# FFN of a hybrid decoder layer in five wider token tiles, with w_down streamed through a ring of four blocks in place of staying in SBUF

## The chip, the cores and the metric

One Trainium2 chip, one program on all 8 cores; each core works on one of the 8 prompts and 16 of the 128 sample tokens, and reads all weights itself. The time is device microseconds of the slowest core. A run is called slow when the cores of one die are over 1% longer than those of the other at a lower clock, or when it is over 1.5% above the fastest of the same kernel; none is used, in the medians either. A ratio is the mean time of one kernel's fast runs over that of the other's fast runs of the same rounds, so it is not quite the ratio of the medians that are quoted beside it. The same kernel moved by up to 3 us between rounds, so two kernels of different rounds are compared by their ratios.

## The reference, cut to what matters (the comment is added)

```python
D_MODEL, D_FF, CONV_W = 1024, 2816, 3          # 2064 own tokens a core go through the FFN tiles
...
    # channel-mixing sub-layer: gated ConvFFN
    h = rmsnorm(x, g_pre_ffn)
    upc, new_ffn = causal_dwconv(h @ w_up, buf_ffn, w_ffn_conv)       # (B,T,2*D_FF)
    gate, val = jnp.split(upc, 2, axis=-1)
    y = (jax.nn.silu(gate) * val) @ w_down
    x = x + rmsnorm(y, g_post_ffn)
```

## The kernel before

A first stage (pooling and convolution mixers, 5 tiles "A") leaves h2, the normed input of the FFN, in a scratch tensor `h2T` in memory. The FFN (the layer's feed-forward part: w_up, a gate, w_down) takes 6 tiles of 344 tokens. A tile has 22 `pair`s (gate and value block of w_up, 2 x 8 matmuls of 346 columns, then convolution, silu and product) and 8 `wdown` blocks (22 matmuls each), which run one tile later, between the pairs of the next tile. All of w_down, 8 blocks of bf16, stays in SBUF, the core's on-chip memory, over the space of dead mixer weights. The weights are float32 in memory and bf16 in SBUF, so each of their loads is a casting DMA, issued from POOL. The outputs of all tiles but the last are added to what `yT` in memory holds, by accumulating stores from POOL. (The code is cut and its comments are added.)

```python
    W_DN = Buf(W_POOL.off, 8, FC * 128, True)      # 8 resident blocks
    H2W = NB + 8
    bl = Alloc(W_DN.end)
    h2a = bl(KC, H2W, True)                        # first h2 buffer, over two chunks of the pooled buffer
    TB = [bl(2, NB), bl(2, NB)]
    g0 = bl(FC, NB, True)
    ...
    def load_h2(t):
        lo = T0B + t * NB - 2
        hb = H2[t % 2]
        sp_dma(hb.ap[:, :, 0:NBH], h2T[:, :, lo:lo + NBH],
               [("h2", a, q) for a in tiles_a(lo, lo + NBH) for q in range(2)], [hb.t()], 128 * KC * NBH * 2)
    ...
    def wload(buf, src, m, after=()):              # float32 in memory, bf16 in SBUF: a casting DMA from POOL
        rows, per = buf.n // src.shape[0], src.shape[2]
        return pool_dma(buf.flat[:, m * per:(m + 1) * per], src[m], [], [buf.t(m * rows, rows)], 128 * per * 4, mx=2048,
                        after=after)
    ...
    for t in range(NTB):
        ...
        for j in range(FC):
            pair(t, j)
            if t == 0:
                wup(1)                             # one more block of w_up
            ...
            if (t, j) in ((0, 9), (0, 11), (0, 14), (0, 16), (0, 19), (0, 21), (1, 1), (1, 3)):
                wdn()                              # one w_down block, 8 in all
            wd = WD1 if t == 1 else WD
            if t > 0 and j in wd:
                wdown(t - 1, wd[j])
            if t > 1 and j == 0:
                epi_y(t - 2)                       # norm of a finished tile, accumulating stores to yT
    ...
    for m in range(8):
        wdown(NTB - 1, m, ...)                     # the tail: the last tile's own down-projection
```

A list scheduler inside the program orders the instructions of each engine; each engine has its instructions in that order, and so has the sync engine (SP) its DMAs.

## Time and profile before

| | before |
|---|---|
| time, median of 3 (later 4) runs | 823.04 (823.63) us |
| span of the profiled run, slowest core (the page is of a core of 816.0 us) | 816.4 us |
| PE busy, matmuls | 796.5 us, 5118 |
| w_down loads | 8 |
| transfers over the span | 93 GB/s |

In the page's strip of 40 slices, each digit is a busy share in tenths; PEclk is the granted TensorE clock.

```profile
PE   7999999999999999999999999999999999999994
PEclk9999999999999999999999999999999999999998
DMA  9999706567017699999990132015101500050073
```

### The profile page before, as it was taken

The page shows a single profiled execution, that of the slowest core. Times are in us where ns is not written, and L with a number is a line of the kernel's source. Part 1 is how long each engine was busy: PE and PEld are TensorE (multiplying, and loading weights), DVE is VectorE, ACT ScalarE, POOL GpSimd, SP SyncE. Part 2 cuts the span into 40 slices and gives each one's busy share as a digit, 9 for nine tenths or more (in the row PEclk, how much of TensorE's full clock was granted, in tenths as well). Part 3 has the DMA queues.
Part 4 walks back from the last instruction along what each step waited for, and adds up shares of the span by engine and source line. Part 5 has one row for each costly group of instructions (what it writes and reads, how often), then busy time and mean ns, then how long its engine had stood idle before and what let it go on. Part 6 is the DMA issues. An engine that isn't in the chain of part 4 may idle for free.

```text
span 816.0 us, 16713 instructions; the slowest of 8 cores (813.3 to 816.4 us)
## 1 busy us (share of the span) xinstructions
PE 796.5 (98%) x5118; PEld 498.2 (61%) x5118; DVE 562.4 (69%) x1056; ACT 451.9 (55%) x903; POOL 258.7 (32%) x296
## 2 busy tenths in 40 slices
PE   7999999999999999999999999999999999999994
PEld 5454455555555555666666666666666666666663
DVE  3897547886977687488886486568566765785732
ACT  3433375665465644676754475456556554765532
POOL 6542002001201243599432252225222522242231
PEclk9999999999999999999999999999999999999998
DMA  9999706567017699999990132015101500050073
GB/s 183 203 159 156 153 10 139 159 165 155 25 56 158 106 142 190 172 160 176 183 159 3 36 44 54 0 37 71 37 2 36 70 1 1 2 71 2 1 147 82
DMA packets 64006, 75.51 MB, mean 93 GB/s; under 512 B 3088, under 2 KB 59536, under 8 KB 63904
## 3 DMA queue, kind: packets, MB, share of 16 engines
q0 software_dynamic: 41168, 44.61, 38.8%
q1 hardware_dynamic: 22752, 29.84, 12.8%
q8 instruction: 43, 0.70, 0.3%
q14 instruction: 43, 0.35, 0.2%
HBM read 81.89 MB, written 22.90 MB: 128 GB/s over the span
## 4 chain that ended last, share of the span: by engine, by line
PE 94%; DMA 2%; DVE 1%; issue 1%; ACT 1%; DVEq 0%; POOL 0%; SPq 0%; ACTq 0%; POOLq 0%
PE ps L469 94%; DMA big<-w_in 1%; DMA big<-xT 1%; DVE big L549 0%; DVE big L821 0%; ACT big L817 0%; POOL big L482 0%; DVEq L1077 0%; ACT big L958 0%; DVE big L658 0%; DVE ps L869 0%; SPq L476 0%; DVE big L869 0%; DVE big L880 0%; DVE big L664 0%
## 5 line engine op out<-in xcount | busy, mean ns | idle before, releaser
L469 PE MATMUL ps<-big 128*128 128x346 bf16 (+5 forms) x5118 | 796.5, 319 | 9.0 <-DVE big L821 2.0
L469 PEld LDWEIGHTS ps<-big 128*128 128x128 bf16 x5118 | 498.2, 98 | 307.1 <-issue 12.9
L821 DVE SCALAR_TENSOR_TENSOR big<-ps,big 128x344 f32<-128x344 f32 (+1 forms) x528 | 281.1, 569 | 97.2 <-ACT big L817 75.1
L835 POOL TENSOR_TENSOR big<-big 128x344 bf16<-128x344 f32 x132 | 125.5, 952 | 259.2 <-DVE big L821 175.7
L817 ACT ACTIVATE big<-ps,big 128x344 f32<-128x344 f32 (+1 forms) x264 | 140.1, 541 | 71.3 <-PE ps L469 67.1
L834 ACT ACTIVATE big<-big 128x344 f32<-128x344 f32 x132 | 64.5, 489 | 44.2 <-DVE big L821 41.9
L700 ACT ACTIVATE big<-ps 128x392 f32<-128x392 f32 (+1 forms) x80 | 39.3, 513 | 55.5 <-PE ps L469 35.8
L480 POOL DMA_DIRECT2D big<-xT x16 | 14.9, 941 | 162.1 <-DVE big L713 148.6
L847 ACT ACTIVATE big<-ps,big 128x344 f32<-128x344 f32 x48 | 26.0, 546 | 55.5 <-PE ps L469 54.2
L482 POOL DMA_DIRECT2D big<-w_up x44 | 31.8, 727 | 53.3 <-PE ps L469 47.1
L713 DVE SCALAR_TENSOR_TENSOR big<-ps,big 128x392 f32<-128x392 f32 (+1 forms) x40 | 25.8, 645 | 31.2 <-PE ps L469 29.0
L509 DVE TENSOR_TENSOR big<-big 128x1568 bf16<-128x1568 bf16 (+3 forms) x28 | 23.6, 847 | 30.8 <-ACT big L732 28.9
L853 DVE TENSOR_TENSOR big<-big 128x688 bf16<-128x688 bf16 x17 | 8.8, 517 | 40.7 <-ACT big L850 40.7
L730 ACT ACTIVATE big<-ps,big 128x392 f32<-128x392 f32 (+1 forms) x40 | 24.5, 611 | 13.6 <-PE ps L469 13.5
L606 DVE TENSOR_TENSOR big<-big 128x406 f32<-128x406 f32 (+7 forms) x50 | 29.9, 600 | 1.5 <-ACT big L628 0.2
L480 POOL DMA_DIRECT2D yT<-big x20 | 26.2, 1550 | 12.9 <-DVE big L885 7.3
L482 POOL DMA_DIRECT2D big<-w_in x32 | 23.2, 749 | 20.1 <-DMA big<-w_in 11.5
L850 ACT ACTIVATE big<-ps 128x344 bf16<-128x344 f32 x48 | 21.6, 450 | 13.5 <-PE ps L469 13.5
L575 ACT ACTIVATE big<-big 128x392 f32<-128x392 f32 (+1 forms) x20 | 12.6, 637 | 29.1 <-DVE big L664 29.1
L549 DVE SCALAR_TENSOR_TENSOR big<-big 128x392 bf16<-128x392 f32 (+1 forms) x40 | 24.3, 647 | 5.9 <-ACT big L526 3.6
L578 DVE SCALAR_TENSOR_TENSOR big<-big 128x392 f32<-128x392 f32 (+1 forms) x40 | 25.5, 645 | 2.6 <-ACT big L575 2.1
L719 DVE TENSOR_TENSOR big<-big 128x392 bf16<-128x392 f32 (+1 forms) x40 | 24.7, 627 | 2.0
(62 smaller groups left out, 347.1 us busy)
## 6 DMA issues: line engine op xcount, KB each, us to landing
big<-w_up POOLq DMA_DIRECT2D x44, 256.0 KB, 18.4
big<-w_in POOLq DMA_DIRECT2D x32, 256.0 KB, 21.9
yT<-big POOLq DMA_DIRECT2D x20, 344.0 KB, 6.0
big<-xT POOLq DMA_DIRECT2D x16, 392.0 KB, 7.9
yT<-big SPq DMA_DIRECT2D x8, 784.0 KB, 9.2
big<-w_dn POOLq DMA_DIRECT2D x8, 704.0 KB, 28.6
big<-xT SPq DMA_DIRECT2D x6, 784.0 KB, 6.8
big<-h2T SPq DMA_DIRECT2D x6, 692.0 KB, 4.7
```

Source lines behind the costliest of these rows:

```text
L469: ins = e.matmul(o, lhsT=l, rhs=x, start=(start and i == 0), stop=(stop and i == last))
L480: return S.add("pool", lambda e: e.dma_start(out=out, in_=in_, accum_op=ALU.add, max_dma_last_dim=mx), r, w, dma=True, byts=byts, pri=pri, ...
L482: return S.add("pool", lambda e: e.dma_start(out=out, in_=in_, max_dma_last_dim=mx), r, w, dma=True, byts=byts, pri=pri, after=after)
L578: dve(lambda e, k=k: e.scalar_tensor_tensor(out=cv, in0=p[:, 2 + k + lo:2 + k + N], scalar=cc(C_WC + 4 * k + c), in1=cv, op0=ALU.mult, op1 ...
L606: dve(lambda e, nx=nx, cur=cur, s=s, a2=a2: e.tensor_tensor(out=nx[:, a2:W], in0=cur[:, a2:W], in1=cur[:, a2 - s:W - s], op=ALU.add), [ct] ...
L700: act(lambda e, b=b, g=g: e.activation(out=GT[t].ap[:, g, lo:N], in_=bank(b, N, lo), func=AF.Sigmoid), [("ps", b)], [GT[t].t(g, 1)], N, ps ...
L713: dve(lambda e: e.scalar_tensor_tensor(out=A_, in0=bank(bp, N, lo), scalar=cc(C_PS + m), in1=A_, op0=ALU.mult, op1=ALU.mult), [("ps", bp), ...
L817: act(lambda e, b=b, fj=fj, tt=tt: e.activation(out=tt[:, 0:n], in_=bank(b, n), func=AF.Copy, scale=cc(C_WF + fj)), [("ps", b), KCST], [to ...
L821: dve(lambda e, b=b, fj=fj, tt=tt, k=k: e.scalar_tensor_tensor(out=tt[:, 0:n], in0=ps[:, b * 512 + k:b * 512 + k + n], scalar=cc(C_WF + 44 ...
L834: act(lambda e: e.activation(out=g, in_=g, func=AF.Silu), [T.t(0, 1)], [T.t(0, 1)], NB, tab="silu")
L835: S.add("pool", lambda e: e.tensor_tensor(out=gb.ap[:, j, :], in0=g, in1=v, op=ALU.mult), [T.t()], [gb.t(j, 1)], dur=NB * 2.17 + 100)
L847: act(lambda e: e.activation(out=Y.ap[:, m, :], in_=bank(b, NB), func=AF.Copy, scale=cc(C_G4 + m)), [("ps", b), KCST], [Y.t(m, 1)], NB, ps ...
```

## The change

Its intent: fewer, wider matmuls (448 columns of a PSUM bank, which has 512 in this kernel), fewer fixed costs on all engines, and a short last tile so that the tail is short. The wider buffers fit only if w_down gives up half of its place: it passes through a ring of 4 blocks, a block's slot being filled with the block four further on as soon as its matmuls end. The last five blocks of the last tile go to five extra places, over w_up blocks that the last tile no longer needs. The core of the diff (cut: `N` for `NB` in many places, small temporaries moved, the h2 operations of the last A tile moved from pairs 20 to 29 to pairs 14 to 21):

```diff
-NTB = 6
-NB = 344
+TB_N = (448, 448, 448, 448, 272)
+OB = (0, 448, 896, 1344, 1792)
+NTB = 5
+NB = 448
...
-    W_DN = Buf(W_POOL.off, 8, FC * 128, True)
+    ring = Alloc(W_POOL.off)
+    W_DN = [ring(1, FC * 128, True) for _ in range(NR)]          # NR = 4
+    W_DNX = [Buf(W0 + 3 * BW * i, 1, FC * 128, True) for i in range(5)]
+    bl = Alloc(ring.o)
+    TB = [bl(2, NB)]
+    Y = bl(KC, NB)
+    TB.append(bl(2, NB))
     h2a = bl(KC, H2W, True)                    # now over three chunks of the pooled buffer
...
+    def wdn_buf(s):
+        return W_DN[s % NR] if s < 8 * NTB - 5 else W_DNX[s - (8 * NTB - 5)]
+
+    def wdn_load(s):
+        if s < 8 * NTB:
+            wload(wdn_buf(s), w_dn[s % 8:s % 8 + 1], 0, after=[last_pe[0]])
...
     def wdown(t, m, mid=None):
...
+        if s + NR < 8 * NTB - 5:                # s = 8 * t + m
+            wdn_load(s + NR)
...
+            if t == 0 and j in (12, 14, 16, 18):
+                wdn_load((j - 12) // 2)
+            if t == NTB - 1 and j in (7, 9, 11, 13, 15):
+                wdn_load(8 * NTB - 5 + (j - 7) // 2)
```

More of the change, by code (lines that the diff above doesn't have):

```diff
@@ L27 @@
 SCA = NA - NS
-NTB = 6
-NB = 344
-NBH = NB + 2
-SCB = NB - NS
+TB_N = (448, 448, 448, 448, 272)
+OB = (0, 448, 896, 1344, 1792)
+NTB = 5
+NB = 448
+NBL = TB_N[-1]
 T0B = 16
@@ L34 @@
 LOP = LO - 2
-SBW = 53200
+SBW = 53208
 GR = 4
@@ L377, in build_nc @@
     o_sq2 = al(KC, NMX, True).off
-    TMPF = al(4, NS)
+    al.o = SBW - 200 - 8 * NS
     STG = al(1, 200)
@@ L381, in build_nc @@
     assert al.o <= SBW, al.o
-    X = per_tile(KC, False, [o_x, W_O.off] + [o_x] * 3)
+    X = per_tile(KC, False, [o_x, W_O.off] + [o_cv + 5 * NA + 32] * 3)
     R = per_tile(KC, False, [o_r] + [X[2].end] * 4)
@@ L395, in build_nc @@
     PT = [Buf(o_pt, 2, UW), Buf(CV[1].end, 2, NA + 16)] + [Buf(CV[2].end, 2, NA + 16)] * 3
-    assert PT[2].end <= F_END and BGCV[1].end <= U.off and PT[1].end <= R[0].end
+    assert PT[2].end <= X[2].off and BGCV[1].end <= U.off and PT[1].end <= R[0].end
     ST_POOL = Buf(o_h2s, 4, 15 * NS)
@@ L410, in build_nc @@
     NMID = 12
+    NR = 4
     W_UP = Blocks([W0 + BW * i for i in range(16)] + [U.off + BW * i for i in range(NMID)] +
@@ L413, in build_nc @@
     assert U.off + BW * NMID <= F_END
-    W_DN = Buf(W_POOL.off, 8, FC * 128, True)
     H2W = NB + 8
-    bl = Alloc(W_DN.end)
+    ring = Alloc(W_POOL.off)
[5 more added lines that the diff above has]
+    TB.append(bl(2, NB))
     h2a = bl(KC, H2W, True)
-    TB = [bl(2, NB), bl(2, NB)]
     g0 = bl(FC, NB, True)
-    assert g0.end <= U.off
+    assert h2a.off >= MERGED[4].end and g0.end <= U.off, (h2a.off, g0.end)
     bl = Alloc(U.off + BW * NMID)
     g1 = bl(FC, NB, True)
-    Y = bl(KC, NB)
     YSQ = bl(4, NB, True)
     TB.append(Buf(SD.off + NMX, 2, NB))
-    bl = Alloc(max(bl.o, XSQ2[4].end))
+    TB.append(bl(2, NB))
+    TB.append(bl(2, NB))
+    assert bl.o <= XSQ2[4].end
+    bl = Alloc(XSQ2[4].end)
     h2b = bl(KC, H2W, True)
     PRE = bl(44, NS)
-    TB.append(bl(2, NB))
+    assert PRE.end <= STG.off
     H2, G = [h2a, h2b], [g0, g1]
@@ L432, in build_nc @@
     assert ST_FFN.end <= PRE.off and R[1].end <= ST_FFN.off + 1600
-    TAIL = Buf(h2a.off, 1, 44 * 18)
-    X1 = Buf(g0.off, KC, NB)
-    assert X1.end <= g0.end
+    TAIL = Buf(h2b.off, 1, 44 * 18)
+    X1 = Buf(g1.off, KC, NBL)
+    YB = [Y] * (NTB - 1) + [Buf(U.off, KC, NBL)]
+    assert X1.end <= g1.end
+    wd_use = [0]
+    def wdn_buf(s):
[3 more added lines that the diff above has]
+            wload(wdn_buf(s), w_dn[s % 8:s % 8 + 1], 0, after=[last_pe[0]])
     def cc(col, n=1):
@@ L613, in pool_c @@
                                              op0=ALU.mult, op1=ALU.subtract), [ct, U.t(c, 1)], [pd.t(c, 1)], N, stt=True)
-        tm = TMPF.ap[:, c, :]
+        tm = RED.ap[:, c, :]
         if t == 0 and w > LO:
@@ L617, in pool_c @@
                                           in1=CST[:, C_IC + 16 * c + lo:C_IC + 16 * c + 16],
-                                          op=ALU.mult), [ct, KCST], [TMPF.t(c, 1)], NS)
+                                          op=ALU.mult), [ct, KCST], [RED.t(c, 1)], NS)
             dve(lambda e: e.tensor_tensor(out=po[:, lo:16], in0=tm[:, lo:16], in1=u[:, 16 + lo:32], op=ALU.subtract),
-                [TMPF.t(c, 1), U.t(c, 1), pd.t(c, 1)], [pd.t(c, 1)], NS)
+                [RED.t(c, 1), U.t(c, 1), pd.t(c, 1)], [pd.t(c, 1)], NS)
         if last:
-            dve(lambda e: e.tensor_tensor(out=tm, in0=RED.ap[:, c, :], in1=u[:, 16 + SCA:W], op=ALU.add),
-                [RED.t(c, 1), U.t(c, 1)], [TMPF.t(c, 1)], NS)
+            dve(lambda e: e.tensor_tensor(out=tm, in0=tm, in1=u[:, 16 + SCA:W], op=ALU.add),
+                [RED.t(c, 1), U.t(c, 1)], [RED.t(c, 1)], NS)
             dve(lambda e: e.scalar_tensor_tensor(out=po[:, SCA:NA], in0=tm, scalar=1.0 / w, in1=u[:, 16 + SCA:W],
                                                  op0=ALU.mult, op1=ALU.subtract),
-                [TMPF.t(c, 1), U.t(c, 1), pd.t(c, 1)], [pd.t(c, 1)], NS)
+                [RED.t(c, 1), U.t(c, 1), pd.t(c, 1)], [pd.t(c, 1)], NS)
         else:
@@ L794, in load_h2 @@
     def load_h2(t):
-        lo = T0B + t * NB - 2
+        lo, n = T0B + OB[t] - 2, TB_N[t] + 2
         hb = H2[t % 2]
-        sp_dma(hb.ap[:, :, 0:NBH], h2T[:, :, lo:lo + NBH],
-               [("h2", a, q) for a in tiles_a(lo, lo + NBH) for q in range(2)], [hb.t()], 128 * KC * NBH * 2)
+        sp_dma(hb.ap[:, :, 0:n], h2T[:, :, lo:lo + n],
+               [("h2", a, q) for a in tiles_a(lo, lo + n) for q in range(2)], [hb.t()], 128 * KC * n * 2, pri=-15000.0)
     set_rr = [0]
@@ L804, in pair @@
         hb, gb = H2[t % 2], G[t % 2]
-        T = TB[set_rr[0] % (3 if t == 0 else 4)]
+        T = TB[set_rr[0] % (3 if t < 2 else 5)]
         set_rr[0] += 1
-        n = SCB if last else NB
+        N = TB_N[t]
+        n = N - NS if last else N
         hv = []
@@ L812, in pair @@
             wb = W_UP.ap(blk).rearrange("p (k c) -> p k c", k=KC)
-            pe([(bank(b, NBH), wb[:, k, :], hb.ap[:, k, 0:NBH]) for k in range(KC)], [W_UP.t(blk), hb.t()],
-               [("ps", b)], NBH)
+            pe([(bank(b, N + 2), wb[:, k, :], hb.ap[:, k, 0:N + 2]) for k in range(KC)], [W_UP.t(blk), hb.t()],
+               [("ps", b)], N + 2)
             hv.append((b, half * FC + j, T.ap[:, half, :], T.t(half, 1)))
@@ L817, in pair @@
             act(lambda e, b=b, fj=fj, tt=tt: e.activation(out=tt[:, 0:n], in_=bank(b, n), func=AF.Copy, scale=cc(C_WF + fj)),
-                [("ps", b), KCST], [tok], NB, psum=True, ap=1)
+                [("ps", b), KCST], [tok], N, psum=True, ap=1)
         for k in (1, 2):
@@ L822, in pair @@
                     out=tt[:, 0:n], in0=ps[:, b * 512 + k:b * 512 + k + n], scalar=cc(C_WF + 44 * k + fj), in1=tt[:, 0:n],
-                    op0=ALU.mult, op1=ALU.add), [("ps", b), tok, KCST], [tok], NB, stt=True)
+                    op0=ALU.mult, op1=ALU.add), [("ps", b), tok, KCST], [tok], N, stt=True)
         if last:
@@ L826, in pair @@
                 dve(lambda e, b=b, fj=fj, tt=tt: e.scalar_tensor_tensor(
-                    out=tt[:, SCB:NB], in0=ps[:, b * 512 + 2 + SCB:b * 512 + NBH], scalar=cc(C_WF + 88 + fj),
+                    out=tt[:, n:N], in0=ps[:, b * 512 + 2 + n:b * 512 + N + 2], scalar=cc(C_WF + 88 + fj),
                     in1=PRE.ap[:, fj, :], op0=ALU.mult, op1=ALU.add), [("ps", b), PRE.t(), KCST], [tok], NS, stt=True)
@@ L830, in pair @@
                 act(lambda e, b=b, fj=fj: e.activation(out=TAIL.ap[:, 0, 18 * fj:18 * fj + 18],
-                                                       in_=ps[:, b * 512 + SCB:b * 512 + NBH], func=AF.Copy),
+                                                       in_=ps[:, b * 512 + n:b * 512 + N + 2], func=AF.Copy),
                     [("ps", b), tok], [("tail", fj)] + ([TAIL.t()] if j == 0 else []), 18, psum=True)
-        g, v = T.ap[:, 0, :], T.ap[:, 1, :]
-        act(lambda e: e.activation(out=g, in_=g, func=AF.Silu), [T.t(0, 1)], [T.t(0, 1)], NB, tab="silu")
-        S.add("pool", lambda e: e.tensor_tensor(out=gb.ap[:, j, :], in0=g, in1=v, op=ALU.mult),
-              [T.t()], [gb.t(j, 1)], dur=NB * 2.17 + 100)
+        g, v = T.ap[:, 0, 0:N], T.ap[:, 1, 0:N]
+        act(lambda e: e.activation(out=g, in_=g, func=AF.Silu), [T.t(0, 1)], [T.t(0, 1)], N, tab="silu")
+        S.add("pool", lambda e: e.tensor_tensor(out=gb.ap[:, j, 0:N], in0=g, in1=v, op=ALU.mult),
+              [T.t()], [gb.t(j, 1)], dur=N * 2.17 + 100)
     def wdown(t, m, mid=None):
@@ L840, in wdown @@
         b = next_bank()
-        wb = W_DN.ap[:, m, :].rearrange("p (k c) -> p k c", k=FC)
+        N = TB_N[t]
+        s, Y = 8 * t + m, YB[t]
+        wt = wdn_buf(s)
+        wb = wt.flat.rearrange("p (k c) -> p k c", k=FC)
         for k0, k1 in ((0, 20), (20, 21), (21, 22)) if t == NTB - 1 and m == 0 else ((0, FC),):
-            pe([(bank(b, NB), wb[:, k, :], gb.ap[:, k, :]) for k in range(k0, k1)], [W_DN.t(m, 1), gb.t(k0, k1 - k0)],
-               [("ps", b)], NB, start=k0 == 0, stop=k1 == FC)
+            pe([(bank(b, N), wb[:, k, :], gb.ap[:, k, 0:N]) for k in range(k0, k1)], [wt.t(), gb.t(k0, k1 - k0)],
+               [("ps", b)], N, start=k0 == 0, stop=k1 == FC)
@@ L845, in wdown @@
+        if s + NR < 8 * NTB - 5:
+            wdn_load(s + NR)
         if mid:
             mid()
-        act(lambda e: e.activation(out=Y.ap[:, m, :], in_=bank(b, NB), func=AF.Copy, scale=cc(C_G4 + m)),
-            [("ps", b), KCST], [Y.t(m, 1)], NB, psum=True, ap=1)
-        s = m if m < 2 else 2 + m % 2
-        act(lambda e: e.activation(out=YSQ.ap[:, s, :], in_=bank(b, NB), func=AF.Square), [("ps", b)], [YSQ.t(s, 1)], NB,
+        act(lambda e: e.activation(out=Y.ap[:, m, 0:N], in_=bank(b, N), func=AF.Copy, scale=cc(C_G4 + m)),
+            [("ps", b), KCST], [Y.t(m, 1)], N, psum=True, ap=1)
@@ L851, in wdown @@
+        r = m if m < 2 else 2 + m % 2
+        act(lambda e: e.activation(out=YSQ.ap[:, r, 0:N], in_=bank(b, N), func=AF.Square), [("ps", b)], [YSQ.t(r, 1)], N,
             psum=True)
         if m in (3, 5) or (m == 7 and t < NTB - 1):
-            dve(lambda e: e.tensor_tensor(out=YSQ.ap[:, 0:2, :], in0=YSQ.ap[:, 0:2, :], in1=YSQ.ap[:, 2:4, :], op=ALU.add),
-                [YSQ.t()], [YSQ.t(0, 2)], 2 * NB, rate=2.0)
+            dve(lambda e: e.tensor_tensor(out=YSQ.ap[:, 0:2, 0:N], in0=YSQ.ap[:, 0:2, 0:N], in1=YSQ.ap[:, 2:4, 0:N],
+                                               op=ALU.add), [YSQ.t()], [YSQ.t(0, 2)], 2 * N, rate=2.0)
@@ L856, in epi_y @@
     def epi_y(t):
+        N, Y = TB_N[t], YB[t]
         if t == NTB - 1:
-            sums([(YSQ, 3, 1)], NB, start=False)
+            sums([(YSQ, 3, 1)], N, start=False)
         else:
-            sums([(YSQ, 0, 2)], NB)
-        ln_exp(0, NB, ps_out=True)
-        sdb = bank(SB, NB).unsqueeze(1).to_broadcast([128, 2, NB])
-        lo = T0B + t * NB
+            sums([(YSQ, 0, 2)], N)
+        ln_exp(0, N, ps_out=True)
+        sdb = bank(SB, N).unsqueeze(1).to_broadcast([128, 2, N])
+        lo = T0B + OB[t]
@@ L866, in epi_y @@
             for i, (k, n, b, _) in enumerate(steps):
-                yk = Y.ap[:, k:k + n, :]
-                out = yk if b is None else ps[:, b * 512:(b + n) * 512].rearrange("p (c n) -> p c n", c=n)[:, :, 0:NB]
+                yk = Y.ap[:, k:k + n, 0:N]
+                out = yk if b is None else ps[:, b * 512:(b + n) * 512].rearrange("p (c n) -> p c n", c=n)[:, :, 0:N]
                 dve(lambda e, yk=yk, out=out, n=n: e.tensor_tensor(
-                    out=out, in0=yk, in1=bank(SB, NB).unsqueeze(1).to_broadcast([128, n, NB]), op=ALU.mult),
-                    [Y.t(k, n), ("ps", SB)], [Y.t(k, n)] if b is None else [("ps", b + r) for r in range(n)], n * NB,
+                    out=out, in0=yk, in1=bank(SB, N).unsqueeze(1).to_broadcast([128, n, N]), op=ALU.mult),
+                    [Y.t(k, n), ("ps", SB)], [Y.t(k, n)] if b is None else [("ps", b + r) for r in range(n)], n * N,
@@ L872, in epi_y @@
                     pri=-80000.0 + 8000 * i)
             for k, n, b, how in steps:
-                yk, xk = Y.ap[:, k:k + n, :], X1.ap[:, k:k + n, :]
+                yk, xk = Y.ap[:, k:k + n, 0:N], X1.ap[:, k:k + n, :]
                 if how == "pool":
                     pool_tt(lambda e, yk=yk, xk=xk: e.tensor_tensor(out=yk, in0=yk, in1=xk, op=ALU.add),
-                            [Y.t(k, n), X1.t(k, n)], [Y.t(k, n)], n * NB)
+                            [Y.t(k, n), X1.t(k, n)], [Y.t(k, n)], n * N)
@@ L878, in epi_y @@
                 else:
-                    src = ps[:, b * 512:(b + n) * 512].rearrange("p (c n) -> p c n", c=n)[:, :, 0:NB]
+                    src = ps[:, b * 512:(b + n) * 512].rearrange("p (c n) -> p c n", c=n)[:, :, 0:N]
                     dve(lambda e, yk=yk, xk=xk, src=src: e.tensor_tensor(out=yk, in0=src, in1=xk, op=ALU.add),
-                        [("ps", b + r) for r in range(n)] + [X1.t(k, n)], [Y.t(k, n)], n * NB)
-                sp_dma(yT[:, k:k + n, lo:lo + NB], yk, [Y.t(k, n)], [("yo", t, k)], 128 * n * NB * 4)
+                        [("ps", b + r) for r in range(n)] + [X1.t(k, n)], [Y.t(k, n)], n * N)
@@ L883, in epi_y @@
+                sp_dma(yT[:, k:k + n, lo:lo + N], yk, [Y.t(k, n)], [("yo", t, k)], 128 * n * N * 4)
             return
         for q in range(4):
-            dve(lambda e, q=q: e.tensor_tensor(out=Y.ap[:, 2 * q:2 * q + 2, :], in0=Y.ap[:, 2 * q:2 * q + 2, :],
+            dve(lambda e, q=q: e.tensor_tensor(out=Y.ap[:, 2 * q:2 * q + 2, 0:N], in0=Y.ap[:, 2 * q:2 * q + 2, 0:N],
                                                in1=sdb, op=ALU.mult),
-                [Y.t(2 * q, 2), ("ps", SB)], [Y.t(2 * q, 2)], 2 * NB)
@@ L888, in epi_y @@
-            pool_dma(yT[:, 2 * q:2 * q + 2, lo:lo + NB], Y.ap[:, 2 * q:2 * q + 2, :],
-                     [Y.t(2 * q, 2)] + [("y", a, q // 2) for a in tiles_a(lo, lo + NB)], [("yo", t, q)],
-                     2 * 128 * 2 * NB * 4, acc=True, mx=4096)
+                [Y.t(2 * q, 2), ("ps", SB)], [Y.t(2 * q, 2)], 2 * N)
+            pool_dma(yT[:, 2 * q:2 * q + 2, lo:lo + N], Y.ap[:, 2 * q:2 * q + 2, 0:N],
+                     [Y.t(2 * q, 2)] + [("y", a, q // 2) for a in tiles_a(lo, lo + N)], [("yo", t, q)],
+                     2 * 128 * 2 * N * 4, acc=True, mx=4096)
@@ L1028, in build_nc @@
     WD1 = {9: 0, 11: 1, 13: 2, 15: 3, 17: 4, 19: 5, 20: 6, 21: 7}
-    EPX = (20, 21, 22, 23, 25, 26, 28, 29)
-    dn = [0]
-    def wdn():
-        if dn[0] < 8:
-            wload(W_DN, w_dn, dn[0], after=[last_pe[0]])
-            dn[0] += 1
+    EPX = (14, 15, 16, 17, 18, 19, 20, 21)
     for t in range(NTB):
@@ L1048, in build_nc @@
                 epi_x(L, EPX.index(22 * t + j))
-            if (t, j) in ((0, 9), (0, 11), (0, 14), (0, 16), (0, 19), (0, 21), (1, 1), (1, 3)):
-                wdn()
+            if t == 0 and j in (12, 14, 16, 18):
+                wdn_load((j - 12) // 2)
+            if t == NTB - 1 and j in (7, 9, 11, 13, 15):
+                wdn_load(8 * NTB - 5 + (j - 7) // 2)
             wd = WD1 if t == 1 else WD
@@ L1063, in build_nc @@
     sp_dma(o_ffn_tail, TAIL.ap[:, 0, :], [("tail", j) for j in range(44)] + [TAIL.t()], ["o8"], 128 * 792 * 4)
-    lo = T0B + (NTB - 1) * NB
-    sp_dma(X1.ap, yT[:, :, lo:lo + NB], [("y", a, q) for a in tiles_a(lo, lo + NB) for q in range(2)],
-           [X1.t()], 128 * KC * NB * 4)
+    lo = T0B + OB[NTB - 1]
+    sp_dma(X1.ap, yT[:, :, lo:lo + NBL], [("y", a, q) for a in tiles_a(lo, lo + NBL) for q in range(2)],
+           [X1.t()], 128 * KC * NBL * 4)
     for m in range(8):
@@ L1069, in build_nc @@
         if m == 6:
-            sums([(YSQ, 0, 3)], NB, stop=False)
+            sums([(YSQ, 0, 3)], NBL, stop=False)
     epi_y(NTB - 1)
```

## The prediction

> **What bounds the kernel now.** I read the engine totals and the chain that ended last first. The kernel's last stage, the FFN, is what the change touches.
>
> ```profile
> PE 796.5 (98%) x5118; PEld 498.2 (61%) x5118; DVE 562.4 (69%) x1056; ACT 451.9 (55%) x903; POOL 258.7 (32%) x296
> ...
> PE 94%; DMA 2%; DVE 1%; issue 1%; ACT 1%; DVEq 0%; POOL 0%; SPq 0%; ACTq 0%; POOLq 0%
> ```
>
> TensorE (PE) carries 94% of the chain. All cores have a mean clock of 0.994 to 0.997, so no throttle is there to be won back. A busy PE need not be a full PE, so I counted matmuls in undisturbed stretches (columns: stretch, its length, then busy us and instructions of PE, PEld, DVE, ACT, POOL; clock; DMA share; GB/s).
>
> ```profile
> 200.00:250.00 50.00, 50.00 (x304) 29.48 (x302) 41.55 (x69) 30.11 (x60) 5.61 (x4) 1.00 0.18 57
> ...
> 436.00:512.00 76.00, 76.00 (x522) 50.83 (x520) 49.76 (x91) 41.60 (x82) 23.58 (x25) 1.00 0.22 36
> 512.00:589.00 77.00, 77.00 (x528) 51.47 (x527) 51.68 (x95) 43.52 (x86) 24.45 (x26) 1.00 0.22 38
> ```
>
> 77.00/528 is 145.8 ns for each FFN matmul. One FFN tile has 352 up matmuls of 346 columns and 176 down matmuls of 344, 345.3 on average; at 2.4 columns per ns that is 143.9 ns, so 1.9 ns of a matmul is fixed cost. At 392 columns (first row) 164.5 ns less 163.3 leaves 1.2 ns. The FFN is already at PE's streaming rate but for 1%.
>
> Then I looked for PE gaps after the start-up. There is one place, the end of the first FFN tile (which starts near 338 us):
>
> ```profile
> 373.00:378.00 5.00, 5.00 (x36) 3.33 (x34) 4.58 (x10) 3.25 (x7) 4.98 (x6) 1.00 1.13 145
> 378.00:383.00 5.00, 5.00 (x37) 3.33 (x35) 3.48 (x7) 2.86 (x7) 4.98 (x4) 1.00 1.16 149
> 383.00:388.00 5.00, 5.00 (x36) 3.22 (x33) 4.36 (x9) 4.10 (x8) 5.00 (x6) 1.00 1.19 254
> 388.00:393.00 5.00, 3.33 (x23) 2.18 (x23) 5.00 (x10) 2.39 (x6) 2.70 (x4) 1.00 1.08 141
> ```
>
> POOL is full (4.98 of 5) from about 353 to 388 us, the three tile buffers TB come back late, and PE then idles 1.7 us. From 390 us the chain is PE without a break to 805.1 us. The end, 805.1 to 816.4 us, is the last tile's norm and its stores. So only three things can move the time: the columns and fixed cost of FFN matmuls, that 1.7 us, and the 11.3 us tail; plus any new stall.
>
> **What the Trainium skill says.** "TensorE: Matmul & The Clock Gate", section Back-to-back issue gap, puts an isolated matmul's warm gap at N/2.4 + 2.5 ns: time goes with columns, and widening saves only the constant. The trace agrees in kind, with 1.9 and 1.2 ns. "VectorE: DVE Perf Modes", section on the TRN2 errata, says VectorE pays a fixed extra per instruction, so wider tiles amortize it. The trace agrees: 572 ns at 344 columns and 556 ns at 328 give about 1.04 ns a column and 214 ns fixed. "DMA: Bandwidth & Descriptors", section SWDGE vs HWDGE vs iDMA, says a DMA that casts must be issued from GpSimd. That fits here: w_down is float32 in memory and bf16 in SBUF, and all its loads are on POOL. So the extra loads cost POOL time.
>
> **The change part by part.**
>
> *FFN matmuls.* Before: 2112 of 346 columns at 146.1 ns and 1056 of 344 at 145.2 ns, 308.6 + 153.3 = 461.9 us. After, with the same 1.9 ns: up, 1408 of 450 columns at 189.4 ns and 352 of 274 at 116.1 ns, 266.7 + 40.9 us; down, 704 of 448 at 188.6 ns and 176 of 272 at 115.2 ns, 132.8 + 20.3 us; 460.7 us. The columns are nearly the same (2076 to 2074 for up, 2064 unchanged), 528 matmuls go: **-1.2 us**, all on the path.
>
> *VectorE, ScalarE, POOL per pair.* One scalar_tensor_tensor goes from 572 to about 680 ns (104 columns more), but 88 of 528 go, so VectorE loses 88 x 0.214 = 19 us of work, ScalarE and POOL some too. All lies beside PE: worth nothing by itself. A full pair needs 4 x 0.66 = 2.65 us of VectorE (instructions start some 18 ns earlier than their duration says: 36 in 19.96 us in a full run) against 16 x 0.189 = 3.03 us of PE, 87%, where it was 2.22 of 2.34 us, 95%.
>
> *First FFN tile.* POOL before: 22 products x 0.93, 8 epilogue operations x 1.85, 13 w_up issues x 0.74, 6 w_down issues x 0.93 us: 20.5 + 14.8 + 9.6 + 5.6 = 50.5 us in 22 x 16 x 0.146 = 51.4 us of PE: full. After: a product of 448 columns takes about 0.93 + 104 x 2.13 ns = 1.15 us (slope from 1628 ns at 688 and 897 ns at 344), so 25.3 + 14.8 + 9.6 + 3.7 (4 ring loads) = 53.4 us in 66.7 us: 80%. The lag should not build up: **-1.5 us**. The eight h2 operations moved from pairs 20 to 29 to pairs 14 to 21 bring VectorE in tile 0 and the first nine pairs of tile 1 to about 31 x 2.65 + 8 = 90 us of 94 us of PE: just in.
>
> *The ring.* 32 more w_down loads, 704 KB written and twice that read. In the FFN, DMA goes from the 36 GB/s above to about 36 + 5.8 MB/100 us = 94 GB/s; this core moved 254 GB/s in the 383 to 388 us row. A load is issued when its slot's matmuls end, four down-projections ahead: 30 to 50 us before its use. Unloaded landing I estimate at 6 to 9 us (accumulating stores of 344 KB land in a median 6.8 us; the 22 to 32 us of today's w_down loads are their queue behind w_up). The tightest is the last ring block: its slot frees at the seventh down-projection of tile 3, and it is used after two short pairs (3.7 us), one 448-column block (22 x 0.189 = 4.15 us) and two 272-column ones (5.1 us), 12.9 us later. **0**, at worst 1 to 3 us. The 32 issues of 0.93 us on POOL lie beside its 50 to 60% idle time.
>
> *Last tile, 272 columns.* A pair there takes 16 x 0.116 = 1.86 us of PE; VectorE needs 4 x 0.46 + 2 x 0.21 = 2.27 us, 122%, where the last tile before needed about 2.57 us against 2.34, 110%. Before the first down-projection (pair 5) there are five such pairs, and the four multiplications of tile 2's output (864 ns at 688 columns, about 1.08 us at 896): 11.4 + 4.3 = 15.7 us of VectorE in 9.3 us of PE. Seven PSUM banks hide 3.5 pairs, 6.5 us. That is on the edge; **+1 us** expected, 0 to 3. After that each down-projection of tile 3 gives PE 4.15 us with no VectorE work, so the lag closes.
>
> *Tail.* After the last down matmul: two ScalarE norm steps and evictions, 72 columns less at about 0.85 ns, x4, 0.25 us; five multiplications and three additions on VectorE, most of 688 columns, become 544 (-0.15 us each), about 0.7 us on the chain; smaller last stores 0.1 us: **-1.0 us**.
>
> Sum: -1.2 - 1.5 + 1 - 1.0 = -2.7 us, **820 us** from 823.
>
> **Rivals.** (1) *The ring starves PE*: a load that lands late stops a down-projection, eight times a tile. For it: 8 cores read 1.4 MB blocks at once, accumulating stores share the POOL queue, and POOL issues in order behind products. Against it: 30 us and more of lead, and a DMA share of 0.22 today. 32 loads late by 1 us each would make 850 us; I give it 3%. (2) *VectorE becomes the bound* in the first tile (96% by my sum) or the last (122%). It would show as PE idle behind the scalar_tensor_tensor line, 3 to 8 us: 823 to 828 us. (3) *The wide tile pays much more than the sum*: if the fixed cost of a matmul were really on PE in a way the counts miss, 528 matmuls x 10 ns would make 5 us, 815 us. The counts at 346 and 392 columns speak against it. (4) *Bigger buffers collide*: Y, g1 and h2 lie over space of the earlier stage, and X, R shift by 88 words. I find each old user finished well before; a miss would cost a few us at the start of the FFN.
>
> **Range and chances.** The gain is capped: PE's own work falls by 1.2 us, gap and tail together hold at most about 3 us more. 2% is 16.5 us, so faster by that is all but impossible. Slower by 2% needs rival 1 or several stalls together. The three runs before spread from 820.75 to 824.92 us, so noise alone is 2 us either way. Range 814 to 828.
>
> **What would show each step.** PE: 4590 matmuls in all, busy near 795 us, and about 189 ns a matmul in mid-FFN; well over 191 ns is a miss. First tile: no stretch with POOL full, no PE idle over 0.5 us there. Ring: 40 w_down loads, landing under 12 us in mid-FFN, no PE wait behind w_down. Last tile: PE idle behind the scalar_tensor_tensor line in the last tile's first six pairs, 0 to 3 us. Tail: some 10.3 us from the last down matmul to the end. The prediction is wrong if PE waits for w_down at all often, or if PE idles over 5 us in the FFN.

## The result, and the profile after

843.09 us median (842.6 to 843.72, 4 runs) against 823.63: ratio 1.0242, 95% interval 1.0213 to 1.0271. The change is slower by over 2%, where the prediction gave 820 us and a range to 828.

First the page of the kernel after: engine totals, the strip, and the chain that ended last.

```profile
PE 799.7 (95%) x4588; PEld 447.8 (53%) x4588; DVE 551.6 (66%) x961; ACT 434.3 (52%) x817; POOL 278.6 (33%) x302
...
PE   7999999999999999599999999999999999999845
...
PEclk9999999999999999799999999999999999999968
DMA  9999717566107899997912448576467764499957
...
PE 88%; DMA 9%; DVE 1%; ACT 1%; issue 1%; DVEq 0%; SPq 0%; ACTq 0%; POOLq 0%
PE ps L486 88%; DMA big<-w_dn 4%; DMA big<-h2T 3%; DMA big<-w_in 1%; DMA big<-xT 1%; DVE big L566 0%; ACT L537 0%; ACT big L982 0%; DVEq L1096 0%; ACT big L537 0%; DVE big L800 0%; DVE big L675 0%; DVE ps L893 0%; ACT big L554 0%; DVE big L730 0%
```

PE's work is as before but transfers have entered the chain: 4% of 841.2 us behind w_down, 3% behind h2T. The strip shows two dents in PE, in the 17th slice and in the last three, each with a dent in PEclk. The DMA line is now busy through the whole second half and full at its end.

Next the timeline of PE from the FFN on (start us, length, what, idle before it and who ended that). An unbroken run of matmuls is one line.

```profile
347.34 445.74 PE L486 MATMUL ps<-big 128*128 128x450 bf16 x2474 [9.32 <-DMA big<-h2T]
795.98 2.71 PE L486 MATMUL ps<-big 128*128 128x272 bf16 x22 [2.90 <-DMA big<-w_dn]
811.13 20.86 PE L486 MATMUL ps<-big 128*128 128x272 bf16 x159 [12.44 <-DMA big<-w_dn]
```

From here on there are three stalls over 1 us and no more: 9.3 us before the first FFN matmul, then 2.9 and 12.4 us in the tail, before the first and second down-projection of the last tile (a down-projection has 22 matmuls). Between them, 445.74 us without a gap. Two windows after the stalls and one in mid-FFN (length, PE, PEld, DVE, ACT, POOL busy us and instructions, clock, DMA share, GB/s):

```profile
347.00:352.00 5.00, 4.66 (x15) 1.99 (x16) 0.67 (x1) 0.63 (x1) 0.00 (x0) 0.57 1.10 141
...
480.00:560.00 80.00, 80.00 (x424) 41.29 (x422) 49.69 (x74) 41.23 (x68) 30.59 (x28) 1.00 0.68 99
...
812.00:817.00 5.00, 5.00 (x29) 3.42 (x27) 0.00 (x0) 0.87 (x3) 0.00 (x0) 0.65 0.05 7
```

Mid-FFN runs at 80.00/424 = 188.7 ns a matmul, as predicted. After each long stall the clock is near half. The Trainium skill ("TensorE: Matmul & The Clock Gate", Part 1) says the array falls to half clock after an idle window of some 3.4 us and needs a busy one to come back; the trace agrees: the waits of 9.3 and 12.4 us were each followed by slow matmuls, the one of 2.9 us was not (22 matmuls in 2.71 us). By count, 15 matmuls in 4.66 us (311 ns) in place of 189 ns lost about 1.8 us; after the tail stall the first 24 matmuls, nearly all of 272 columns, took 5.22 us (217 ns) in place of 115 ns each, about 2.4 us.

So the loss is 9.3 + 1.8 us at the start of the FFN and 15.3 + 2.4 us in the tail, 28.8 us. Less the gain of 3 to 5 us of the wide tiles, that is the 24.8 us between the two spans (841.2 and 816.4).

**The first stall.** Here is the issue of the first tile's h2 load in the timeline of SP, before:

```profile
314.99 0.54 SPq L476 DMA_DIRECT2D big<-h2T  x1
```

and after, where a store of h2 goes ahead of it:

```profile
322.64 0.37 SPq L493 DMA_DIRECT2D h2T<-big  x1
323.16 1.40 SPq L493 DMA_DIRECT2D big<-h2T  x1
```

The same loads in the view of DMA issues of 300 to 348 us (KB, us from issue to landing), before:

```profile
big<-h2T SPq DMA_DIRECT2D x1, 692.0 KB, 17.2
```

and after:

```profile
big<-h2T SPq DMA_DIRECT2D x1, 900.0 KB, 24.0
```

It goes out 8.2 us later, is 30% larger and needs 6.8 us more beside the w_up loads. Before, it landed near 332 us, 6 us ahead of need; after, near 347 us, 9 us late. Two things held its issue back. The buffer lies over three chunks of the pooled buffer in place of two, which are read until a later merge step; and a store of h2 now stands ahead of it in SP's list, which waited for VectorE until 322.57 us. The first experiment takes both away, but the kept trace tells how they stood. The program fixes which semaphore signal of PE the load waits for, the last matmul that reads the chunks: the 289th before, which came at 314.82 us, and the 297th after, which came at 322.45 us. So the place of the buffer alone held the load for 7.6 us longer (0.7 of it because all of this core's work is that much later here), and the store added 0.1 us on this core (0.4 at most on any of the eight).

**The second stall.** The view of DMA issues from 734 to 812 us of the kernel after, and its queue totals (packets, MB, share of 16 engines):

```profile
q0 software_dynamic: 13452, 10.34, 101.5%
...
big<-w_dn POOLq DMA_DIRECT2D x12, 704.0 KB, 25.1
yT<-big POOLq DMA_DIRECT2D x3, 448.0 KB, 14.4
```

Twelve w_down loads are issued during the last tile: seven into the ring, and the five for the extra places. With the accumulating stores they fill all 16 engines for 78 us at 10.34/78 = 133 GB/s, and a load lands 25 us after its issue, where the median over the kernel is 9.6 us. The first block of the tail is issued at 768.2 us, wanted at 793.1 and lands at 795.6; the second is issued at 776.0, wanted at 798.7 and lands at 811.0.

### The profile page after: what moved, and what is told of

It reads as the page before. It is cut to its first block, busy times and chain, and to the rows that moved or that the text cites. A ratio compares the mean times of both kernels' runs of the same rounds, so it can differ in the third digit from the quotient of the medians.

```text
span 841.2 us, 15132 instructions; the slowest of 8 cores (833.7 to 841.2 us)
## 1 busy us (share of the span) xinstructions
PE 799.7 (95%) x4588; PEld 447.8 (53%) x4588; DVE 551.6 (66%) x961; ACT 434.3 (52%) x817; POOL 278.6 (33%) x302
## 4 chain that ended last, share of the span: by engine, by line
PE 88%; DMA 9%; DVE 1%; ACT 1%; issue 1%; DVEq 0%; SPq 0%; ACTq 0%; POOLq 0%
PE ps L486 88%; DMA big<-w_dn 4%; DMA big<-h2T 3%; DMA big<-w_in 1%; DMA big<-xT 1%; DVE big L566 0%; ACT L537 0%; ACT big L982 0%; DVEq L1096 0%; ACT big L537 0%; DVE big L800 0%; DVE big L675 0%; DVE ps L893 0%; ACT big L554 0%; DVE big L730 0%
## 5 line engine op out<-in xcount | busy, mean ns | idle before, releaser
L486 PE MATMUL ps<-big 128*128 128x392 bf16 (+7 forms) x4588 | 799.7, 338 | 32.9 <-DMA big<-w_dn 15.3
L486 PEld LDWEIGHTS ps<-big 128*128 128x128 bf16 x4588 | 447.8, 99 | 384.6 <-issue 40.5
L839 DVE SCALAR_TENSOR_TENSOR big<-ps,big 128x448 f32<-128x448 f32 (+1 forms) x440 | 269.5, 641 | 115.3 <-ACT big L835 96.5
L853 POOL TENSOR_TENSOR big<-big 128x448 bf16<-128x448 f32 (+1 forms) x110 | 119.0, 1092 | 204.0 <-DVE big L839 144.2
L835 ACT ACTIVATE big<-ps,big 128x448 f32<-128x448 f32 (+1 forms) x220 | 129.0, 599 | 80.3 <-PE ps L486 74.4
L852 ACT ACTIVATE big<-big 128x448 f32<-128x448 f32 (+1 forms) x110 | 60.1, 547 | 50.3 <-DVE big L839 48.4
L870 ACT ACTIVATE big<-ps,big 128x448 f32<-128x448 f32 (+1 forms) x40 | 24.2, 604 | 92.0 <-PE ps L486 92.0
L499 POOL DMA_DIRECT2D big<-w_dn x40 | 37.8, 945 | 35.9 <-PE ps L486 33.1
L876 DVE TENSOR_TENSOR big<-big 128x896 bf16<-128x896 bf16 (+1 forms) x14 | 8.4, 599 | 39.8 <-ACT big L873 39.8
L909 DVE TENSOR_TENSOR big<-big,ps 128x896 f32<-128x896 f32 x16 | 16.9, 1079 | 25.0 <-ACT ps L540 25.0
L800 DVE SCALAR_TENSOR_TENSOR big<-big 128x392 bf16<-128x392 f32 (+1 forms) x40 | 27.1, 711 | 1.3 <-ACT big L540 1.3
L566 DVE SCALAR_TENSOR_TENSOR big<-big 128x392 bf16<-128x392 f32 (+1 forms) x40 | 24.3, 646 | 5.4 <-ACT big L543 3.4
## 6 DMA issues: line engine op xcount, KB each, us to landing
big<-w_in POOLq DMA_DIRECT2D x32, 256.0 KB, 22.7
```

What stands on the lines that cost most here:

```text
L486: ins = e.matmul(o, lhsT=l, rhs=x, start=(start and i == 0), stop=(stop and i == last))
L499: return S.add("pool", lambda e: e.dma_start(out=out, in_=in_, max_dma_last_dim=mx), r, w, dma=True, byts=byts, pri=pri, after=after)
L800: dve(lambda e: e.scalar_tensor_tensor(out=h, in0=r, scalar=cc(C_G3 + k), in1=SD.ap[:, rs, lo:N], op0=ALU.mult, op1=ALU.mult), [R[t].t(k, ...
L835: act(lambda e, b=b, fj=fj, tt=tt: e.activation(out=tt[:, 0:n], in_=bank(b, n), func=AF.Copy, scale=cc(C_WF + fj)), [("ps", b), KCST], [to ...
L839: dve(lambda e, b=b, fj=fj, tt=tt, k=k: e.scalar_tensor_tensor(out=tt[:, 0:n], in0=ps[:, b * 512 + k:b * 512 + k + n], scalar=cc(C_WF + 44 ...
L852: act(lambda e: e.activation(out=g, in_=g, func=AF.Silu), [T.t(0, 1)], [T.t(0, 1)], N, tab="silu")
```

## The experiments

My theory after reading the traces: two separate stalls, a late h2 load and too many w_down bytes in the last tile, each made worse by the clock. Rivals: the ring of four is too shallow whatever the volume; the wide tile is slow in itself; the short tile alone makes the stall.

**x1, h2 buffer moved.** Only the places of two buffers change; h2a now ends before the pooled buffer begins. (Asserts are left out of this cut.)

```diff
     Y = bl(KC, NB)
-    TB.append(bl(2, NB))
+    bl = Alloc(GT[4].end)
     h2a = bl(KC, H2W, True)
+    TB.append(bl(2, NB))
```

> The kernel after, with the first h2 buffer moved so that it no longer lies over the pooled buffer; its load can go out some 10 us or more earlier. If the 9.3 us PE wait at the start of the FFN is only a late load, the wait is gone, the half-clock stretch after it (about 2.6 us lost) too, and the time falls by 12 us to about 831 us; the 15.3 us wait behind w_down in the tail stays. Rival, the load is slow because the w_up loads hold the transfer engines: an earlier issue gains less than half of it, 837 us or more. Rival, the wide tile is slow by itself: no change, 843 us.

832.05 us median against 820.89 us of the kernel before in the same rounds, ratio 1.0134 (1.0110 to 1.0159). Both early h2 loads are now out by 287 us. The stall at the start of the FFN is gone, and PE runs on from 48.01 us until the tail:

```profile
48.01 735.37 PE L487 MATMUL ps<-big 128*128 128x392 bf16 x4160 [0.53 <-DVE big L676]
...
801.20 21.57 PE L487 MATMUL ps<-big 128*128 128x272 bf16 x159 [14.11 <-DMA big<-w_dn]
```

The medians fall by 11 us, near the 12 expected, but the kernel before was 2.7 us faster in these rounds too: by the ratios (1.0242 and 1.0134) the fall is some 9 us, as between the two spans (841.2 and 832.0). The start-up of this profiled core ended 2.0 us later, which hides the rest of the 9.3 + 1.8 us. The w_down wait stays (14.1 us). First part shown.

**x2, five loads fewer in the last tile** (wrong result), on the kernel after.

```diff
-            if t == NTB - 1 and j in (7, 9, 11, 13, 15):
-                wdn_load(8 * NTB - 5 + (j - 7) // 2)
```

> The kernel after without the last five w_down loads (wrong result on purpose: the last five down-projections of the last tile use old up weights). The seven ring loads of the last tile stay as they are. If the tail wait is the volume of loads in the last tile (twelve of 704 KB in some 55 us), the 15.3 us wait behind w_down and the half clock after it (2.8 us) go: about 825 us. Rival, the ring of four is too shallow, each load simply takes too long after its slot frees: the three ring loads used in the tail still come late, 838 us or more.

Of six runs three were slow; the fast ones are 823.24, 825.78 and 825.07 us, ratio 1.0043 (1.0014 to 1.0072). PE waits for no w_down at all, though the program has the seven ring loads in the same places:

```profile
345.00 467.31 PE L486 MATMUL ps<-big 128*128 128x450 bf16 x2655 [7.15 <-DMA big<-h2T]
```

The longest landing of a w_down load is 15.2 us, where it was 35.0. So the ring's depth alone is not the matter; the number of loads in the stretch is.

**x3, serpentine order.** Every second tile runs its down-projections from block 7 to block 0, so the four blocks left in the ring are the next ones wanted; the last two tiles share four of the extra places. 20 loads in place of 40, the result right.

```diff
-    def wdown(t, m, mid=None):
+    def wdown(t, p, mid=None):
+        m = p if t % 2 == 0 else 7 - p
...
-        if s + NR < 8 * NTB - 5:
-            wdn_load(s + NR)
+        if p < 4 and t < NTB - 2:
+            wdn_load(t, p + 4 if t % 2 == 0 else 3 - p)
...
-            if t == NTB - 1 and j in (7, 9, 11, 13, 15):
-                wdn_load(8 * NTB - 5 + (j - 7) // 2)
+            if t == NTB - 1 and j in (2, 4, 6, 8):
+                wdn_load(NTB - 1, 3 - (j - 2) // 2)
```

> The kernel after with the down-projections of every second tile in reverse order, so that the four blocks left in the ring are used again: 20 w_down loads in place of 40, 4 in the last tile in place of 12, result right. Volume theory: same gain as without the last five loads, about 825 us. Ring-too-shallow rival: the ring loads of each tile still come four blocks ahead, waits stay, 835 us or more.

Two runs were slow; the two fast ones are 825.79 and 824.98 us, too few for an interval, and just what the volume theory said. The profile has no wait for w_down; the h2 stall stays (8.0 us).

**x4, both mends** (x1 and x3 together).

> Both mends together. If the two waits and the half clock after each are the whole loss (9.3 + 2.6 + 15.3 + 2.8 = 30 us), about 813 us, below the kernel before by 1 per cent; by the prediction's own sum without the stall in the last tile (-1.2 - 1.5 - 1.0) 820 us. If the wide tile or the ring costs something spread over the FFN, over 824 us.

815.9 us median of the fast runs (815.3, 815.9, 817.17; one slow run left out) against 820.89: ratio 0.9939 (0.9912 to 0.9966). The result is right, and it is faster than both kernels, than the kernel before by 0.6%, clear of noise. Its profiled span is 813.8 us against the 841.2 us of the kernel after. My lower figure, 813 us, took the whole 30 us from 843 and is missed by 3 us: the half clock had been put at 5.4 us where the counts above give 4.2, and the profile has a new gap of 1.6 us. The 820 us of the prediction's sum is missed by 4 us on the other side. PE's timeline:

```profile
46.19 685.12 PE L486 MATMUL ps<-big 128*128 128x392 bf16 x3810 [0.53 <-DVE big L675]
732.89 71.44 PE L486 MATMUL ps<-big 128*128 128x274 bf16 x529 [1.58 <-ACT big L848]
```

One gap is left, 1.58 us in the ninth pair of the short last tile. Behind it stands ScalarE, which sat idle 4.65 us before an eviction of Y, waiting for an accumulating store to have read it.

**x5, ring loaded once** (x1, and none of the later loads; wrong result).

```diff
-        if s + NR < 8 * NTB - 5:
-            wdn_load(s + NR)
...
-            if t == NTB - 1 and j in (7, 9, 11, 13, 15):
-                wdn_load(8 * NTB - 5 + (j - 7) // 2)
```

> The first mend (h2 buffer moved) with the ring loaded once and never again: 4 w_down loads in all (wrong result on purpose). What is left is the wider tile alone. If the loads cost nothing but the tail wait, the same as both mends together, 815 to 818 us. If 36 loads cost POOL or transfer time spread over the FFN, some us less than with both mends, 813 or below. If the wide tile itself were bad, over 820 us.

814.83 us median (one slow run left out) against 820.75: ratio 0.9934 (0.9914 to 0.9954). This is the worth of the wide tiles alone, some 5 us of 821. By the ratios it is within 1 us of x4 with its 20 loads (0.9934 and 0.9939): away from the last tile, the loads cost no time that these runs can see.

**x6, the tile of 272 third** in place of last (on x1; all 40 loads stay).

```diff
-TB_N = (448, 448, 448, 448, 272)
-OB = (0, 448, 896, 1344, 1792)
+TB_N = (448, 448, 272, 448, 448)
+OB = (0, 448, 896, 1168, 1616)
```

> The first mend with the tile of 272 third in place of last; all 40 loads stay, in the same number for each tile. Volume theory: twelve loads now have the up-projections of 448 columns to hide in (about 100 us in place of 75) and the 14 us wait behind w_down in the tail is gone; the tail is some 1.5 us longer: 832 - 14 - 2.8 + 1.5, about 817 us. Rival, the tail itself asks for blocks faster than a ring can give, whatever came before: a wait of several us stays, 824 us or more.

818.32 us median against 820.75, ratio 0.9980 (0.9957 to 1.0002); 832 became 818. PE waits for no w_down. Here are the w_down loads of 710 to 800 us, where the tail begins, to be read beside the 25.1 us above:

```profile
big<-w_dn POOLq DMA_DIRECT2D x8, 704.0 KB, 9.0
```

The window has eight of the twelve loads; the other four went out from 692 to 709 us. The loads are the same in number; with a last tile of 448 columns to hide in, they land in 9 us. So a tail as such does not ask for blocks too fast; but this one also asks more slowly, 4.1 us a block (22 x 188.6 ns) in place of 2.5. That the tail of 272 columns can be served as well is shown by x2.

**x7, a bf16 copy** (on x1). The first eight loads cast as before and are written back once as bf16; the other 32 read that copy through SP's queue without a cast.

```diff
+    wdb = nc.dram_tensor("wdb", [8, 128, FC * 128], BF16).ap()
...
-        if s < 8 * NTB:
+        if s < 8:
             wload(wdn_buf(s), w_dn[s % 8:s % 8 + 1], 0, after=[last_pe[0]])
+            sp_dma(wdb[s], wdn_buf(s).flat, [wdn_buf(s).t()], [("wdb", s)], 128 * FC * 128 * 2)
+        elif s < 8 * NTB:
+            sp_dma(wdn_buf(s).flat, wdb[s % 8], [("wdb", s % 8)], [wdn_buf(s).t()], 128 * FC * 128 * 2, after=[last_pe[0]])
```

> The first mend, and each w_down block written back once to memory as bf16; all later loads read that copy, half the bytes, from the sync engine's queue without a cast. If what fills the transfers in the last tile is the bytes read from memory (float32, twice what is written), landing there falls to half and the tail wait goes: about 816 to 818 us. If it is the bytes written or the number of packets, the wait stays: 828 us or more.

815.45 us median (one slow run left out) against 820.75: ratio 0.9937 (0.9917 to 0.9958), right result, level with x4. The last tile's transfers, 715 to 800 us:

```profile
q1 hardware_dynamic: 2912, 10.17, 38.8%
...
big<-wdb SPq DMA_DIRECT2D x12, 704.0 KB, 6.4
```

The same twelve blocks take 39% of the engines' time over 85 us in place of all of it over 78. But two things changed at once, the bytes read and the packets: 5632 bytes each in place of 704. x9 and x10 below take the packets alone.

**x8, the ring alone**, on the kernel before (six tiles of 344, 48 loads, the same five extra places).

```diff
-    W_DN = Buf(W_POOL.off, 8, FC * 128, True)
+    W_DN = [ring(1, FC * 128, True) for _ in range(NR)]
+    W_DNX = [Buf(W0 + 3 * BW * i, 1, FC * 128, True) for i in range(5)]
...
-            if (t, j) in ((0, 9), (0, 11), (0, 14), (0, 16), (0, 19), (0, 21), (1, 1), (1, 3)):
-                wdn()
+            if t == 0 and j in (12, 14, 16, 18):
+                wdn_load((j - 12) // 2)
+            if t == NTB - 1 and j in (7, 9, 11, 13, 15):
+                wdn_load(8 * NTB - 5 + (j - 7) // 2)
```

> The kernel before (six tiles of 344) with the ring of four and its five extra places: the ring alone, 48 loads. Its last tile gives the twelve loads nearly the same time as the last tile of the kernel after (77 us against 74 us). Volume theory: the tail waits here too, 4 to 14 us plus a half-clock stretch, 827 to 836 us. Rival, only the short tile makes the wait: 821 to 823 us.

831.82 us median (one slow run left out) against 820.75: ratio 1.0140 (1.0119 to 1.0161), within the expected range. PE's timeline has two waits in the tail here too, before the second and third down-projection:

```profile
788.36 5.04 PE L480 MATMUL ps<-big 128*128 128x344 bf16 x22 [8.31 <-DMA big<-w_dn]
798.03 21.52 PE L480 MATMUL ps<-big 128*128 128x344 bf16 x135 [4.64 <-DMA big<-w_dn]
```

So the second stall does not need the wide tile: the ring with its twelve late loads makes one of 12.9 us by itself.

**x9 and x10, larger packets** (on x1; `wload` passes `mx` on): the w_down loads may use pieces of up to 4096 bytes of a row in memory, or the whole row, in place of 2048.

```diff
-            wload(wdn_buf(s), w_dn[s % 8:s % 8 + 1], 0, after=[last_pe[0]])
+            wload(wdn_buf(s), w_dn[s % 8:s % 8 + 1], 0, after=[last_pe[0]], mx=4096)     # x10: mx=16384
```

> The first mend (h2 buffer moved); the w_down loads may use pieces of up to 4096 bytes of a row in memory in place of 2048, so that a packet writes 1408 bytes in place of 704. In the trace of the kernel after a casting packet of 704 bytes took a median 74 ns and one of 1024 bytes 98 ns: 21 ns fixed and 75 ns for 1000 bytes, so 127 ns for 1408 bytes in place of 148. If the fixed part counts, the 76 us that the last tile's loads take fall by 14 per cent and the 14 us wait by about 10: 820 to 825 us. If only bytes count (cast from float32), 830 to 833 us.

> The same with whole rows, 5632 bytes written by a packet: 443 ns by the same line in place of 592, 25 per cent less. If the fixed part counts, the wait in the tail is gone or nearly: 815 to 820 us, near the run with the bf16 copy. If only bytes count, 830 to 833 us.

x9: 825.64 us median against 820.37, ratio 1.0059 (1.0034 to 1.0084), 0.6 us above the expected range. x10: 819.91 us against 820.37, ratio 0.9991 (0.9968 to 1.0014), within it. The median packets took 126 ns (1408 bytes) and 436 to 440 ns (5632 bytes, by core), where the line through two points had said 127 and 443. On the slowest core of each profile PE still waits 11.7 us (x9) and 4.2 us (x10) for w_down, against 14.1 in x1; the other cores of x9 wait 6.6 to 8.2 us. The loads of x10 from 720 to 800 us:

```profile
q0 software_dynamic: 2816, 10.49, 85.9%
...
big<-w_dn POOLq DMA_DIRECT2D x12, 704.0 KB, 20.7
```

PE's only stall after the start-up that is over 1 us:

```profile
788.23 21.08 PE L487 MATMUL ps<-big 128*128 128x272 bf16 x159 [4.22 <-DMA big<-w_dn]
```

So packet size is a real part of the volume's cost, and one argument of the load call mends most of the tail. The rest, up to the 6.4 us of x7, lies in the packets themselves: one that writes 5632 bytes took a median 436 ns with the cast from POOL's queue (x10) and 215 ns without it from SP's (x7). Whether the cast's double reading or the queue makes the difference no run tells.

## Why the prediction was wrong, point by point

**FFN matmuls, -1.2 us: right.** 4588 matmuls against 5118 (4590 were predicted, a few records can be missing), 188.7 ns in mid-FFN against 189.

**First tile, -1.5 us: right in the time, wrong in the picture.** None of x1, x4 and x5 has a PE gap there. But POOL did not fall to 80% where it had been full: in x4 it is busy 34.67 of 37.00 us from 353 to 390 us, and 11.93 of 30.00 us after that, so the work bunches in the first part of the tile. Why PE is spared all the same was not tested; a pair lasts longer (16 x 189 ns in place of 16 x 146 ns).

**Tail, -1.0 us: about right.** After, 831.7 to 841.2 us, some 9.5 us from the last down matmul; 10.3 had been predicted, from 11.3. The three terms together, -3.7 us, can be checked in x5: 0.9934 of 821 us is -5.4 us, with an interval from -3.8 to -7.1. That agrees, with the wide tile perhaps slightly undervalued.

**Last tile, +1 us: the size is luck, the place and the cause were wrong.** x4 shows 1.58 us, in the ninth pair and not in the first six, and x3 1.57 there. The kernel after, x5 and x7 show none. In x4 ScalarE waits for a store, as said there; PE did not wait for VectorE's arithmetic.

**The ring, "0, at worst 1 to 3 us": the step that failed.** It cost 15.3 us of waiting and about 2.4 us of half clock. Three numbers in it were wrong.
- The load was averaged: 5.8 MB over a tile of 100 us, 94 GB/s. In mid-FFN that was right (99, 76 and 93 GB/s in three stretches of 75 to 80 us, and no wait). But the last tile is 74 us and holds twelve loads, since the five for the extra places fall into the same stretch. My text never counted those five beside the ring's own. 12 x 0.72 MB and three stores are 10 MB in 78 us.
- The capacity was read from one row, 254 GB/s. That row lies near the end of the first FFN tile and is not a stretch of steady casting loads; the other rows of the same view say 141 to 149 GB/s at a DMA share over 1, and they are in my own fence. Casting loads got 133 GB/s at a full queue.
- The landing was taken for an empty queue, 6 to 9 us, against a slack of 12.9 us. With that queue the median was 25.1 us and the longest 35.0. Nor was the block that I took for the tightest, the third of the last tile, the one that PE waited for: the first two, which had leads of 24.9 and 22.7 us, landed in 27.4 and 35.0.

With 10 MB at 133 GB/s, 78 us, the prediction's own slack test would have failed. I had called the 22 to 32 us landings before "their queue behind w_up", and that was the very thing to ask of the new loads: what queue will they stand in?

**Rival 1 was the case, at 3%**, though not as it was pictured: not eight late loads a tile but two late loads in one tail.

**Rival 4, buffers that collide: "each old user finished well before; a miss would cost a few us" failed as well.** My text gives no check of it. The median landing of all h2 loads before, 5.6 us, would have let it pass. But the one that matters runs beside the w_up loads and had taken 17.2 us even before; the larger one took 24.0. The miss cost 9.3 us and about 1.8 us of half clock.

**The clock after a stall was left out.** The stalls of 9.3 and 12.4 us here, and those of 4.2 us in x10 and 4.6 and 8.3 us in x8, were followed by a granted clock of 0.50, the one of 2.9 us was not. Such a stall costs more than its length; here some 4 us of the 28.8.

**Small slips that change nothing.** 572 and 556 ns at 344 and 328 columns give 1.0 ns a column and 228 ns fixed, not 1.04 and 214; at 448 columns the instruction took 681 ns, where about 680 had been said. The 6.8 us for accumulating stores is a median with the xT loads; the stores alone took 6.6.

What stays open: how much of x7's gain over x10 is the cast and how much the queue; and what part the accumulating stores have in the last tile's queue, since no run took them out.

## What to carry to other kernels

Before a resident operand is turned into a stream, lay out its loads along the time line, stretch by stretch, and set the megabytes of each stretch against a rate measured under the same kind of load; a comfortable lead in blocks says nothing when the queue in front of the last block is full. The stretches to fear are those where extra loads, stores and a short tile meet, here the last one. If blocks are reused in cycles, turning the order round on every second pass halves the loads at no cost that these runs show (x4), and paying the cast once and reading back bf16 (x7) does as well: each, with the h2 buffer moved, turned +2.4% into -0.6%.

## What the Trainium skill lacked or had wrong

- "DMA: Bandwidth & Descriptors", Bandwidth, gives 341 GB/s for a 1 MB load from GpSimd, measured on one core with its neighbour idle, and nothing for a load that casts. Here, with eight cores, casting float32 loads with accumulating stores beside them wrote 133 GB/s (10.34 MB in 78 us) at a full queue; bf16 reads by SP used 38.8% of the engines over 85 us for 10.17 MB.
- The same page gives no cost of a packet of a casting load. By bytes written, the medians were 74 ns at 704, 98 at 1024, 126 at 1408 and 436 at 5632: some 21 ns and 74 to 75 ns for 1000 bytes. Without a cast, from SP, a packet of 5632 bytes took 215 ns. Packets of 5632 bytes were the best of the three sizes tried for w_down (832, 826 and 820 us).
- "TensorE: Matmul & The Clock Gate", Back-to-back issue gap, has 2.5 ns of fixed cost a matmul. These traces show 1.9 ns at 344 to 346 columns, 1.2 at 392 and 1.5 at 448 to 450 (188.7 ns less 449.3/2.4).
- No page says how to judge a ring of streamed weights. In x8, 48 loads of 704 KB with a lead of four blocks ran free of waits until twelve of them met in one stretch of 77 us.
